# Gate and up in a fixed order by slots, and the second half of each norm placed further behind the first

## The chip, the cores and the metric

One core of a Trainium2 chip runs the whole kernel. The metric is the time of one execution on the device in microseconds (us); the median of several runs counts. Engines are named as the profile names them: PE is TensorE (the matrix multiplier; PEld its weight loads), DVE VectorE, ACT ScalarE, POOL GpSimd, and SP the engine that issues nearly all transfers (SPq is its queue).

## What is computed

One inference step of an encoder layer on 1024 prompt frames and 32 frames of a running stream (1056 columns in all), in fp32, with D_MODEL 1024:

```
x = x + 1/2 * SwiGLU_1(RMSNorm(x))              # FFN1: gate, up, down
h = RMSNorm(x)
q,k,v of 8 stick-breaking heads; q,k,v,r,gate of 4 GLA heads = h @ w_in
o_sb  = rmsnorm(stick_breaking(rmsnorm(q), rmsnorm(k), v))
o_gla = rmsnorm(gated_linear_attention) * silu(r)
x = x + concat(o_sb, o_gla) @ w_out             # the mixer
x = x + 1/2 * SwiGLU_2(RMSNorm(x))              # FFN2
x = RMSNorm(x)

swiglu(h) = (silu(h @ w_gate) * (h @ w_up)) @ w_down        # D_FF = 2816
```

## The kernel before

Each fp32 operand of a large product is split in two: a rounded part "hi" and a remainder "lo" (`split_to`, L94 on ACT makes hi, L98 on DVE makes lo). A product is then three matmuls, hi·hi, hi·lo and lo·hi.

The program runs in stages: FFN1 (an opening in plain products, then gate and up, then down), the mixer, FFN2 in the same form, and the last norm.

**Gate and up.** `gate_up` runs over 20 `Step`s, gate and up of ten row blocks in turn. A Step is a Strassen-Winograd scheme of seven products, taken in `ORDER = (1, 6, 7, 5, 2, 4, 3)`. One product is 24 matmuls of 128x264 (L378) into one of four PSUM accumulators acc_a to acc_d; `after` takes the accumulators out (L391, L394, L397, L416 to L434), and `form`/`keep` (L442, L451) split the hidden rows into forms that are spilled for the down stage. Beside the products of step t the operands of step t+1 are made: `prep` builds the sums S1 to S4 on POOL (L349 to L362) and splits them, `split_w` splits the first weight block ("whl"). Raw weights come by the transfers of L330 and L331.

In FFN1 alone, `Splits` does a chore beside this: 52 half blocks of the mixer's weights (44 of w_in, 8 of w_out) are loaded (L77, 256 KB), split (L94, L98) and stored (L84, 512 KB) for later use. They go through two buffers in turn, S.x[2] and S.x[3]. `keep` uses S.x[0] and S.x[1] in the same manner. The slot of the chore, one product each, is 7·t+n; half block n is loaded at slot 5n//2, split at +3 and stored at +4.

What sets the order of all this is the scheduler of the Tile framework: it takes the instructions that the program emits, estimates when each can start, and writes each engine's queue in its own order. So a chore that stands after a product in the text can lie ahead of or behind it in a queue. On one engine the queue is then executed strictly in order.

**The mixer.** The attention of head pairs p = 0 to 3 is a list of items into which "filler" work is woven, in the order of the list `fill`: for p < 3 the projections of the next pair (`sb_project`: lists pq, pk, pv of three chunks with eight products each), for p = 3 the output groups (`out_group`). A `Norm` has two parts: `stat` squares the rows and sums them on PE into st; then DVE adds epsilon (nv, L756 and L757), POOL takes the power (nr, L759) and copies the result out over 64 rows (L812). `apply` transposes that on PE (tr, L831) and multiplies (L834). `spread_in` puts the three parts of `stat` into a list, and `apply` is put in some places later.

Of the kernel before, what the change touches and what calls it, by code (L numbers as in the profile page):

```python
# [8 lines left out]
F32 = mybir.dt.float32  # L9
F32R = mybir.dt.float32r  # L10
# [44 lines left out]
class Splits:  # L55
# [3 lines left out]
    def __init__(self, S, jobs, bufs):  # L59
        self.S, self.jobs, self.bufs = S, jobs, bufs  # L60
        self.at = {}
        for n in range(2 * len(jobs)):
# [4 lines left out]
    def buf(self, n):  # L67
        return self.bufs[n % 2][:, :1024]

    def halves(self, n):  # L70
        return self.buf(n).rearrange("p (a n) -> p a n", a=2)

    def cols(self, n):
        return slice(n % 2 * 512, n % 2 * 512 + 512)

    def load(self, n):
        self.S.nc.sync.dma_start(self.buf(n)[:, 512:], self.jobs[n // 2][0][:, self.cols(n)])  # L77

    def split(self, n):
        t = self.halves(n).bitcast(F32R)  # L80
        split_to(self.S, t[:, 0], t[:, 1], self.buf(n)[:, 512:])

    def store(self, n):
        self.S.nc.sync.dma_start(self.jobs[n // 2][1][:, :, self.cols(n)], self.halves(n))  # L84

    def some(self, slot):
        for fn, n in sorted(self.at.pop(slot, ()), key=lambda job: job[1]):
            fn(n)

# [227 lines left out]
class Step:  # L317
# [14 lines left out]

    def split_w(self):
        w = self.S.wp.tile([P, 2, 1024], F32R, name="whl", tag="w")
        split_to(self.S, w[:, 0], w[:, 1], self.raw0)
        self.W["A11"], self.W["A12"] = w[:, :, :512], w[:, :, 512:]

    def prep(self, p, eng):

# [105 lines left out]
    def keep(self, name, src):  # L445

        S = self.S
        S.n_kept = getattr(S, "n_kept", 0) + 1
# [17 lines left out]

def gate_up(S, H, op, steps, among, between, tail, xd, chore):


    N = len(steps)  # L470
    done = {}

    def prep(t, p):
        if t >= N:
            return
        steps[t].prep(p, S.nc.gpsimd if t else S.nc.vector)
        done[t] = done.get(t, 0) + 1
        if done[t] == 5 and t + 2 < N:
            steps[t + 2].load()

    for j in range(4):
        for n, i in enumerate((0, 1, 2, 3) if j < 3 else (0, 2, 1, 3)):
            op.product(j, i, among(j, n))
            between(j, n)
            if i == 2:
                op.silu()
            if j == 3 and n == 1:
                steps[0].split_w()
                for p in (6, 7, 5):
                    prep(0, p)  # L490
        op.store(j)
        if j == 1:
            steps[0].load()
            steps[1].load()
    for k in range(4):
        H.part("T3", k, 1)
    for p in (4, 3):
        prep(0, p)
    for t in range(N):
        for p in ORDER:  # L500
            steps[t].product(p)
            steps[t].after(p)
            n = ORDER.index(p)
            for back, name in FORMS[t % 2].get(n, ()):
                if t >= back:
                    steps[t - back].form(name)
            if p > 2:
                prep(t + 1, p)
            if p == 7 and t < N - 1:
                steps[t + 1].split_w()  # L510
            chore(7 * t + n)
            if t == N - 1:
                if p == 1:
                    for d in range(4):
                        S.nc.sync.dma_start(S.x[d], xd[d])
                tail(p)

# [9 lines left out]
class DownStep:  # L527
# [5 lines left out]

    def prep(self, raw):

# [4 lines left out]
        s34 = S.s32.tile([P, 512], F32, name="s34", tag="s2")  # L540
        s1, s2, s3, s4 = s12[:, :w], s12[:, w:], s34[:, :w], s34[:, w:]
        nc.gpsimd.tensor_add(s1, a[3], a[2])
        nc.gpsimd.tensor_sub(s2, s1, a[0])
        nc.gpsimd.tensor_sub(s3, a[0], a[3])
        nc.gpsimd.tensor_sub(s4, a[1], s2)
        tag = ("S1", "A22") if self.odd else ("S2", "S3")
        wa = S.sr.tile([P, 2, 512], F32R, name=tag[0], tag=tag[0])
# [3 lines left out]
        split_to(S, ws[:, 0, :512], ws[:, 1, :512], s12)  # L551
        split_to(S, wb[:, 0, :w], wb[:, 1, :w], a[2])
        split_to(S, ws[:, 0, 512:], ws[:, 1, 512:], s34)
# [42 lines left out]
class Down:  # L596
# [35 lines left out]
    def prep(self, i):  # L632
        if i < len(self.steps):
            self.steps[i].prep(self.raw.pop(i))

    def head(self, p):
# [4 lines left out]
        elif p == 6:  # L641
            for n in range(4):
                self.load_part(0, n)
        elif p == 7:
            self.load_part(0, 4)
            self.load_part(0, 5)
            self.prep(0)
        elif p == 5:
            self.load_part(0, 6)

    def strassen(self, xd):
# [518 lines left out]
def sb_project(S, A, p, norms=()):  # L1170
# [272 lines left out]
def body(tc, A):  # L1443
# [10 lines left out]
    with ExitStack() as top:  # L1454
# [66 lines left out]
        with ExitStack() as es:  # L1521
# [40 lines left out]
            splits = Splits(S, jobs, (S.x[2], S.x[3]))  # L1562
            gate_up(S, H, op, steps, among, between, down.head, A["x"], splits.some)
            nc.vector.tensor_copy(S.identb, consts[:, 0])
# [18 lines left out]
        with ExitStack() as es:  # L1583
# [61 lines left out]
            with ExitStack() as eg:  # L1645
# [16 lines left out]
                for p in range(4):  # L1662
# [3 lines left out]
                    else:  # L1666
# [33 lines left out]
        with ExitStack() as es:  # L1700
# [67 lines left out]

            gate_up(S, H, op, steps, lambda j, n: [], between, down.head, xs, lambda n: None)
            down.strassen(xs)  # L1770
# [111 lines left out]
```

## Time and profile before

| what | value |
|---|---|
| runs | 2164.31, 2160.37, 2160.37 us |
| median | 2160.37 us |
| the profiled execution's own time | 2163.55 us |
| its span, mean granted PE clock | 2161.8 us, 0.987 |
| PE, DVE, ACT, POOL busy | 2067.5, 1454.9, 887.7, 668.8 us |
| gate and up of FFN1, from acc_a's third matmul to the first of down | 84.47 to 524.47 us |
| gate and up of FFN2 | 1497.27 to 1906.82 us |
| attention and output groups of the mixer, roughly | 1000 to 1395 us |

The durations are those of the one profiled execution, whose time is 3.18 us above the median of the runs. A row of a waits view reads "engine tile line <- engine tile line: us in total, times, longest us": the first waits and the second releases it. A row by windows gives a stretch, its length, and for each engine the busy time in it (with the count of instructions), then the granted PE clock (1.00 is full), the share of the DMA engines and GB/s.

### The profile page before, as it was taken

What the parts mean: (1) busy time and instruction counts of PE and PEld (TensorE: products, weight loads), DVE (VectorE), ACT (ScalarE), POOL (GpSimd) and SP (SyncE); (2) the same over time, 40 slices, a digit from 0 to 9 for tenths busy, and PEclk for the clock granted to TensorE, in tenths of its full rate; (3) what the DMA queues carried; (4) which work ended last, traced back from release to release, by engine and by line L of the source; (5) the groups of instructions that cost most, each with busy time, mean ns of one, the idle gap of its engine ahead of it and who ended that gap; (6) DMA issues with size and microseconds to landing.
All of it is one profiled execution on the core that took longest, in us unless ns stands there. A gap on an engine that the chain in (4) does not pass through costs nothing.

```text
span 2161.8 us, 38696 instructions
## 1 busy us (share of the span) xinstructions
PE 2067.5 (96%) x15636; PEld 1997.3 (92%) x15636; DVE 1454.9 (67%) x2205; ACT 887.7 (41%) x1618; POOL 668.8 (31%) x578
## 2 busy tenths in 40 slices
PE   7999988999999999999999998999999999999997
PEld 6898988999999988888889987899999999999997
DVE  6866677664778556376776677687566666457865
ACT  6543444432223333243654555454333433322333
POOL 0133333444775110011112201101343443458720
PEclk9999999999999999999999999999999999999999
DMA  4277777546854121112133243242334334398322
GB/s 173 81 254 259 262 267 269 204 161 249 339 193 125 69 77 59 63 63 85 37 101 98 78 135 106 85 134 80 120 141 156 142 130 160 129 379 299 108 65 81
DMA packets 128339, 325.03 MB, mean 150 GB/s; under 512 B 12096, under 2 KB 32864, under 8 KB 124832
## 3 DMA queue, kind: packets, MB, share of 16 engines
q1 hardware_dynamic: 128160, 322.56, 42.6%
q8 instruction: 123, 2.02, 0.4%
q14 instruction: 56, 0.46, 0.1%
HBM read 201.72 MB, written 114.03 MB: 146 GB/s over the span
## 4 chain that ended last, share of the span: by engine, by line
PE 69%; DVE 11%; DMA 7%; issue 6%; POOL 4%; ACT 3%; SPq 0%; DVEq 0%; ACTq 0%; POOLq 0%
PE acc_a L378 8%; PE acc_d L378 8%; PE acc_c L378 7%; PE acc L286 4%; PE pj L103 4%; PE acc_b L378 4%; PE pj L105 3%; PE pj L104 3%; PE pd_c L574 3%; PE pd_d L574 3%; PE pd_a L574 3%; PE pd L103 2%; PE pd L105 2%; PE pd L104 2%; DMA win_split<-x 2%
## 5 line engine op out<-in xcount | busy, mean ns | idle before, releaser
L378 PE MATMUL acc_a<-h,whl 128*128 128x264 f32 x1920 | 251.4, 287 | 11.5 <-ACT s L391 9.5
L378 PEld LDWEIGHTS acc_a<-h,whl 128*128 128x128 f32 x1920 | 242.3, 191 | 12.9 <-ACT s L391 10.8
L378 PE MATMUL acc_d<-part,S 128*128 128x264 f32 x1920 | 247.3, 284 | 3.7 <-DVE x L418 3.6
L378 PEld LDWEIGHTS acc_d<-part,S 128*128 128x128 f32 x1920 | 238.7, 188 | 4.7 <-DVE x L418 4.3
L94 ACT ACTIVATE x<-x 128x528 fp32r<-128x528 f32 (+1 forms) x164 | 103.4, 638 | 295.8 <-POOL x L428 81.5
L98 DVE TENSOR_TENSOR x<-x 128x528 fp32r<-128x528 f32 (+1 forms) x164 | 132.1, 814 | 132.7 <-ACT x L94 132.0
L103 PE MATMUL pj<-h,whl 128*128 128x352 f32 x576 | 205.3, 356 | 0.0
L105 PE MATMUL pj<-h,whl 128*128 128x352 f32 x576 | 190.9, 331 | 0.0
L104 PE MATMUL pj<-h,whl 128*128 128x352 f32 x576 | 189.3, 329 | 0.0
L94 ACT ACTIVATE S<-s 128x512 fp32r<-128x512 f32 x160 | 98.2, 623 | 114.7 <-PE acc_d L378 43.1
L428 POOL TENSOR_TENSOR x<-tc,x 128x528 f32<-128x528 f32 x60 | 103.3, 1722 | 123.4 <-DVE tc L427 110.7
L362 POOL TENSOR_TENSOR s<-wraw,s 128x512 f32<-128x512 f32 x38 | 49.8, 1312 | 295.2 <-DVE S L98 295.2
L378 PE MATMUL acc_c<-h,A 128*128 128x264 f32 x960 | 126.7, 288 | 10.1 <-DVE u L397 9.8
L378 PEld LDWEIGHTS acc_c<-h,A 128*128 128x128 f32 x960 | 121.8, 190 | 12.3 <-DVE u L397 12.3
L378 PE MATMUL acc_b<-h,S 128*128 128x264 f32 x960 | 124.7, 285 | 1.5 <-ACT h L94 1.1
L98 DVE TENSOR_TENSOR S<-s,S 128x512 fp32r<-128x512 f32 x160 | 120.8, 756 | 6.3 <-ACT S L94 5.6
L378 PE MATMUL acc_c<-part,S 128*128 128x264 f32 x960 | 123.8, 284 | 1.1 <-DVE hid L298 1.1
L378 PEld LDWEIGHTS acc_b<-h,S 128*128 128x128 f32 x960 | 120.5, 188 | 1.9 <-ACT h L94 1.3
L378 PEld LDWEIGHTS acc_c<-part,S 128*128 128x128 f32 x960 | 119.5, 188 | 1.3 <-DVE hid L298 1.3
L592 POOL TENSOR_TENSOR x<-x,u 128x528 f32<-128x528 f32 x64 | 102.9, 1615 | 49.7 <-DVE x L563 49.4
L103 PEld LDWEIGHTS pj<-h,whl 128*128 128x128 f32 x576 | 110.5, 192 | 5.1 <-issue 1.7
L349 POOL TENSOR_TENSOR s<-wraw 128x512 f32<-128x512 f32 x38 | 51.7, 1360 | 201.4 <-DVE S L98 195.2
(343 smaller groups left out, 4952.3 us busy)
## 6 DMA issues: line engine op xcount, KB each, us to landing
part_spill<-x SPq DMA_DIRECT2D x112, 528.0 KB, 2.8
h<-part_spill SPq DMA_DIRECT2D x64, 528.0 KB, 8.9
part<-part_spill SPq DMA_DIRECT2D x48, 528.0 KB, 9.6
win_split<-x SPq DMA_DIRECT2D x44, 512.0 KB, 4.0
whl<-win_split SPq DMA_DIRECT2D x22, 1024.0 KB, 5.0
wraw<-w1g SPq DMA_DIRECT2D x22, 512.0 KB, 4.8
wraw<-w1u SPq DMA_DIRECT2D x22, 512.0 KB, 4.0
x<-win SPq DMA_DIRECT2D x44, 256.0 KB, 3.6
```

Source lines behind the costliest of these rows:

```text
L94: nc.scalar.activation(hi, src, AF.Copy)
L98: nc.vector.tensor_sub(lo, src, hi.bitcast(F32))
L103: nc.tensor.matmul(out, w[:, 0, wsl], a[:, 0, asl], start=first, stop=False)
L104: nc.tensor.matmul(out, w[:, 0, wsl], a[:, 1, asl], start=False, stop=False)
L105: nc.tensor.matmul(out, w[:, 1, wsl], a[:, 0, asl], start=False, stop=last)
L286: nc.tensor.matmul(out, self.w[i](k, a), quarter(S, k, b, j), start=k == 0 and n == 0, stop=k == KT - 1 and n == 2)
L349: eng.tensor_add(self.s1, a21, a22)
L362: eng.tensor_sub(src, a12, self.s2)
L378: nc.tensor.matmul(t[:, s, :SW], w[:, a, ks], m(k, b, s), start=fresh and k == 0 and n == 0, stop=k == 3 and n == 2, skip_group_check=not ...
L428: nc.gpsimd.tensor_mul(two(hid), t, sg)
L574: nc.tensor.matmul(t[:, s, :SW], w[:, u, k * P : k * P + P], b[:, v, ss(s)], start=fresh and k == 0 and i == 0, stop=k == 1 and i == 2, sk ...
L592: nc.gpsimd.tensor_add(x[r][h], x[r][h], u)
```

## The change

1. `Slots` is new. One slot is one product. `Slots.split` puts hi on ACT (L50) into slot k from now, lo on DVE (L51) one slot later, and what follows, a store, one more later. `Slots.run` is called behind each product's `after`.
2. The loop over the Steps now stands in a `manual_schedule` for PE, DVE, ACT, POOL and SP: there each engine's queue is the order of the text, in FFN1 and FFN2.
3. `prep`, `split_w`, `keep` and `Splits` split through the slots: sums one slot later, whl in the same slot, kept parts one slot later with the store at +3; a half block of the chore is loaded at 5n//2, hi at +2, lo at +3, store at +4.
4. The raw weights of step t+2 are loaded at the second product of step t (those of step 2 ahead of the loop), and no longer when five operands of step t are ready.
5. Down's first step makes its sums at product 7 and its halves at product 2 of the last gate/up step, no longer both at 7.
6. In the mixer `apply` of the norm of a head pair goes from pq[1] to pq[2], that of the further norms from pk[2] to pv[0], that of k stays in pv[2] while its `stat` goes from pv[1] to the middle of pv[0]. At p = 3 `apply` (`turned`) goes one place further on (8 for 7), and the nine `ready` splits stand at every second place from 9, no longer at each one from 10.

```diff
+class Slots:
+    def __init__(self, S):
+        self.S, self.now, self.at = S, 0, {}
+    def later(self, k, fn):
+        self.at.setdefault(self.now + k, []).append(fn)
+    def split(self, hi, lo, src, k, then=None):
+        nc = self.S.nc
+        self.later(k, lambda: nc.scalar.activation(hi, src, AF.Copy))
+        self.later(k + 1, lambda: nc.vector.tensor_sub(lo, src, hi.bitcast(F32)))
+        if then is not None:
+            self.later(k + 2, then)
+    def run(self):
+        for fn in self.at.pop(self.now, ()):
+            fn()
...
 class Splits:
-            slot = 5 * n // 2
-            for k, fn in ((0, self.load), (3, self.split), (4, self.store)):
-                self.at.setdefault(slot + k, []).append((fn, n))
...
+            slots.later(k, lambda buf=buf, src=src, cols=cols: dma(buf[:, 512:], src[:, cols]))
+            slots.split(hl[:, 0], hl[:, 1], buf[:, 512:], k + 2, lambda t=t, out=out, cols=cols: dma(out[:, :, cols], t))
...
-        split_to(S, w[:, 0], w[:, 1], src)
+        split(w[:, 0], w[:, 1], src, 1)
...
-        split_to(S, t[:, 0], t[:, 1], src)
-        S.nc.sync.dma_start(S.parts[self.i - 1, PARTS.index(name)], t.bitcast(F32))
+        S.slots.split(t[:, 0], t[:, 1], src, 1, lambda: S.nc.sync.dma_start(out, t.bitcast(F32)))
...
-        if done[t] == 5 and t + 2 < N:
-            steps[t + 2].load()
...
+    steps[2].load()
+    chores(slots)
+    E = mybir.EngineType
+    with S.tc.manual_schedule(engines={E.PE, E.DVE, E.Activation, E.Pool, E.SP}):
+        for t in range(N):
+            for n, p in enumerate(ORDER):
+                steps[t].product(p)
+                steps[t].after(p)
+                slots.run()
+                for back, name in FORMS[t % 2].get(n, ()):
+                    if t >= back:
+                        steps[t - back].form(name)
+                if t < N - 1:
+                    if p > 2:
+                        steps[t + 1].prep(p, S.nc.gpsimd, slots.split)
+                    if p == 7:
+                        steps[t + 1].split_w(slots.split)
+                        slots.run()
+                if n == 1 and t and t + 2 < N:
+                    steps[t + 2].load()
...
+                slots.now += 1
...
     for n in norms[:1]:
-        spread_in(pq[0], 1, 2, n.stat())
-        pq[1][4:4] = [(4, n.apply)]
+        spread_in(pq[0], 0, 3, n.stat())
+        pq[2][4:4] = [(4, n.apply)]
...
     for n in norms[1:]:
         spread_in(pk[1], 0, 3, n.stat())
-        pk[2][4:4] = [(4, n.apply)]
+        pv[0][2:2] = [(4, n.apply)]
...
-    spread_in(pv[1], 0, 3, [(2, start_k), mean_k(1), mean_k(2)])
-    pv[2][2:2] = [(4, lambda: T.nk.apply())]
+    spread_in(pv[0], 4, 3, [(2, start_k), mean_k(1), mean_k(2)])
+    pv[2][0:0] = [(4, lambda: T.nk.apply())]
...
-                        spread_in(fill, 1, 1, prev.stat() + [(4, turned)])
+                        spread_in(fill, 1, 1, prev.stat())
+                        fill.insert(8, (4, turned))
                         for n in range(9):
-                            fill.insert(10 + n, (1, lambda n=n: ready(n // 3, n % 3)))
+                            fill.insert(9 + 2 * n, (1, lambda n=n: ready(n // 3, n % 3)))
```

Three places show what this does to the queues.

The first is ACT in the second Step of FFN1, before. `x_76<-x_76 128x512` is the hi of a chore half block (or, with 128x528, of a kept part), S2, S3, S1 and whl are operands of the next Step, `s1_1125<-acc_a_1100` takes out the Step's first product.

```order
L94 ACTIVATE x_76<-x_76 128x512
L391 ACTIVATE s1_1125<-acc_a_1100 128x528
L94 ACTIVATE S2_1159<-s2_1157 128x512
L94 ACTIVATE x_76<-x_76 128x512
L94 ACTIVATE S3_1193<-s3_1191 128x512
L94 ACTIVATE x_76<-x_76 128x512
L94 ACTIVATE S1_1228<-s1_1155 128x512
L94 ACTIVATE x_76<-x_76 128x528
L94 ACTIVATE whl_1435<-wraw_1095 128x1024
L94 ACTIVATE x_76<-x_76 128x528
L94 ACTIVATE x_76<-x_76 128x512
```

Changed, the same place reads:

```order
L397 ACTIVATE s1_1120<-acc_a_1095 128x528
L50 ACTIVATE x_76<-x_76 128x512
L50 ACTIVATE S4_1094<-s3_1092 128x512
L50 ACTIVATE x_76<-x_76 128x512
L50 ACTIVATE S2_1159<-s2_1157 128x512
L50 ACTIVATE whl_1197<-wraw_872 128x1024
L50 ACTIVATE S3_1196<-s3_1194 128x512
L50 ACTIVATE S1_1232<-s1_1155 128x512
L50 ACTIVATE x_76<-x_76 128x512
L50 ACTIVATE x_76<-x_76 128x528
L50 ACTIVATE A22_1292<-wraw2_873 128x512
L397 ACTIVATE s1_1351<-acc_a_1326 128x528
```

Before, three chores and a kept part stand ahead of, between and behind S2, S3 and S1, the operands of the third Step, and the whl that follows already belongs to the fourth. Now the third Step's whl is made beside S2, and every slot has one operand and one or two splits that end in a store.

The second is PE at the start of FFN1's gate and up, before. acc_a_876 is the first product of the first Step, with the weights whl; acc_b_904 is the second, with S2.

```order
L378 MATMUL acc_a_876<-h0_84,whl_785 128x264 x2
L378 MATMUL acc_b_904<-h0_84,S2_792 128x264 x3
L378 MATMUL acc_b_904<-h1_85,S2_792 128x264 x3
L378 MATMUL acc_b_904<-h2_86,S2_792 128x264 x3
L378 MATMUL acc_b_904<-h3_87,S2_792 128x264 x3
L378 MATMUL acc_b_904<-h0_84,S2_792 128x264 x3
L378 MATMUL acc_b_904<-h1_85,S2_792 128x264 x3
L378 MATMUL acc_b_904<-h2_86,S2_792 128x264 x3
L378 MATMUL acc_b_904<-h3_87,S2_792 128x264 x3
L378 MATMUL acc_c_938<-part0_104,S3_797 128x264
L378 MATMUL acc_a_876<-h0_84,whl_785 128x264
```

Changed:

```order
L384 MATMUL acc_a_878<-h0_84,whl_785 128x264 x3
L384 MATMUL acc_a_878<-h1_85,whl_785 128x264 x3
L384 MATMUL acc_a_878<-h2_86,whl_785 128x264 x3
L384 MATMUL acc_a_878<-h3_87,whl_785 128x264 x3
L384 MATMUL acc_a_878<-h0_84,whl_785 128x264 x3
L384 MATMUL acc_a_878<-h1_85,whl_785 128x264 x3
L384 MATMUL acc_a_878<-h2_86,whl_785 128x264 x3
L384 MATMUL acc_a_878<-h3_87,whl_785 128x264 x3
L384 MATMUL acc_b_906<-h0_84,S2_792 128x264 x3
```

Two of acc_a's 24 matmuls were followed by all 24 of acc_b before acc_a went on; now all of acc_a stand ahead of acc_b.

The third is DVE in the attention of pair 0, in the norm of the next pair's k, before: from the second nv to the first multiplication kf by the transposed result.

```order
L757 TENSOR_SCALAR nv_11076<-st_10975 32x2
L1314 SCALAR_TENSOR_TENSOR f_11088<-f_11088 128x768
L1315 TENSOR_TENSOR w_11089<-w_11089,f_11088 128x768
L98 TENSOR_TENSOR wt_11055<-tr_11108,wt_11055 128x4x128
L834 SCALAR_TENSOR_TENSOR kf_10787<-kf_10787,vec_70,tr_11138 128x512
```

Changed:

```order
L776 TENSOR_SCALAR nv_10988<-st_10953 32x2
L104 TENSOR_TENSOR wt_10997<-tr_10998,wt_10997 128x128
L1305 TENSOR_TENSOR x_76<-avt_11023,av_11006 64x256
L1333 SCALAR_TENSOR_TENSOR f_11026<-f_11026 128x512
L1334 TENSOR_TENSOR w_11027<-w_11027,f_11026 128x512
L104 TENSOR_TENSOR wt_10997<-tr_11040,wt_10997 128x2x128
L1333 SCALAR_TENSOR_TENSOR f_11048<-f_11048 128x640
L104 TENSOR_TENSOR wt_11067<-tr_11068,wt_11067 128x3x128
L1334 TENSOR_TENSOR w_11049<-w_11049,f_11048 128x640
L1305 TENSOR_TENSOR x_76<-avt_11085,av_11080 64x256
L1333 SCALAR_TENSOR_TENSOR f_11091<-f_11091 128x768
L853 SCALAR_TENSOR_TENSOR kf_10790<-kf_10790,vec_70,tr_11118 128x512
```

Three instructions of the attention lay between the two; now there are ten.

More of the change, by code (lines that the diff above doesn't have):

```diff
@@ L60, in __init__, with plan @@
         self.S, self.jobs, self.bufs = S, jobs, bufs
[L61 to L88 removed]
+    def plan(self, slots):
+        for n in range(2 * len(self.jobs)):
+            k = 5 * n // 2
+            buf = self.bufs[n % 2][:, :1024]
+            t = buf.rearrange("p (a n) -> p a n", a=2)
+            hl = t.bitcast(F32R)
+            src, out = self.jobs[n // 2]
+            cols = slice(n % 2 * 512, n % 2 * 512 + 512)
+            dma = self.S.nc.sync.dma_start
+            slots.later(k, lambda buf=buf, src=src, cols=cols: dma(buf[:, 512:], src[:, cols]))
+            slots.split(hl[:, 0], hl[:, 1], buf[:, 512:], k + 2, lambda t=t, out=out, cols=cols: dma(out[:, :, cols], t))
 def split_to(S, hi, lo, src, pool=False):
@@ L464, in gate_up_steps, with gate_up, prep @@
     return steps
-def gate_up(S, H, op, steps, among, between, tail, xd, chore):
+def gate_up(S, H, op, steps, among, between, tail, xd, chores):
     N = len(steps)
[L471 to L477, printed above, removed]
-        if done[t] == 5 and t + 2 < N:
-            steps[t + 2].load()
+    slots = S.slots = Slots(S)
+    now = lambda hi, lo, src, k: split_to(S, hi, lo, src)
+    def prep(p):
+        steps[0].prep(p, S.nc.vector, now)
     for j in range(4):
@@ L497, in gate_up @@
     for p in (4, 3):
[L498 to L516, printed above, removed]
+        prep(p)
+    steps[2].load()
[18 more added lines that the diff above has]
+                    steps[t + 2].load()
+                if t == N - 1:
+                    if p == 1:
+                        for d in range(4):
+                            S.nc.sync.dma_start(S.x[d], xd[d])
+                    tail(p)
+                slots.now += 1
 PAIRS = [(1, 2), (3, 4), (5, 6), (7, 8)]
@@ L532, in __init__, with sums @@
         self.odd = m % 2
-    def prep(self, raw):
+    def sums(self, raw):
         S, nc = self.S, self.S.nc
@@ L1562, in body @@
             splits = Splits(S, jobs, (S.x[2], S.x[3]))
-            gate_up(S, H, op, steps, among, between, down.head, A["x"], splits.some)
+            gate_up(S, H, op, steps, among, between, down.head, A["x"], splits.plan)
             nc.vector.tensor_copy(S.identb, consts[:, 0])
@@ L1767, in between @@
                     emit(parts(H))
-            gate_up(S, H, op, steps, lambda j, n: [], between, down.head, xs, lambda n: None)
+            gate_up(S, H, op, steps, lambda j, n: [], between, down.head, xs, lambda slots: None)
             down.strassen(xs)
```

25 lines of the change are left out of this document (17 added, 8 removed).

## The prediction

> **What bounds the kernel now.** I read the page first, then the time by windows, then who waits for whom in the windows that fall short. TensorE carries the kernel:
>
> ```profile
> span 2161.8 us, 38696 instructions
> PE 2067.5 (96%) x15636; PEld 1997.3 (92%) x15636; DVE 1454.9 (67%) x2205; ACT 887.7 (41%) x1618; POOL 668.8 (31%) x578
> ```
>
> The change reorders and removes no matmul, so it can win at most what PE idles or runs at a reduced granted clock. Where that lies, the windows tell: gate and up of FFN1 while the chores run, the rest of it, the same work in FFN2, and short stretches around stalls.
>
> ```profile
> core 0: us, PE busy (x) PEld busy (x) DVE busy (x) ACT busy (x) POOL busy (x), PEclk, DMA share, GB/s
> 100.00:377.00 277.00, 254.62 (x2021) 250.22 (x2019) 192.85 (x250) 115.03 (x195) 103.30 (x66) 0.99 0.74 262
> 377.00:495.00 118.00, 117.07 (x959) 117.03 (x960) 73.57 (x95) 43.11 (x70) 49.93 (x33) 1.00 0.48 173
> 1497.27:1906.82 409.55, 409.55 (x3361) 409.55 (x3360) 251.21 (x325) 149.77 (x240) 164.35 (x115) 1.00 0.41 149
> 140.00:145.00 5.00, 3.04 (x17) 3.04 (x18) 4.00 (x7) 3.24 (x7) 1.49 (x2) 0.80 0.68 249
> 230.00:235.00 5.00, 4.32 (x23) 4.33 (x24) 4.95 (x9) 3.36 (x7) 0.00 (x0) 0.68 0.57 219
> 85.00:90.00 5.00, 5.00 (x31) 5.00 (x30) 5.00 (x9) 0.61 (x1) 1.28 (x1) 0.66 0.18 62
> ```
>
> FFN2 is the measure: 3360 matmuls in 409.55 us with no PE idle, 0.1219 us each and 2.925 us for a product of 24 (a slot). At that pace the 2021 matmuls from 100 to 377 take 246.3 us; they took 277.0. Of the 30.7 us lost, 22.4 are idle (277 − 254.6) and 8.3 are matmuls at a reduced clock, as the rows at 140 and 230 show (0.80, 0.68). After the chores the loss is 118 − 959 × 0.1219 = 1.1 us. So the chores cost it. Who waits between 110 and 377:
>
> ```profile
> DVE x L98 <- ACT x L94: 73.9, 33, 4.4
> ACT x L94 <- DMA x<-win: 54.0, 22, 5.9
> ACT x L94 <- POOL x L428: 29.6, 9, 3.7
> PE acc_c L378 <- DVE u L397: 9.8, 8, 2.3
> PE acc_a L378 <- ACT s L391: 9.5, 6, 2.0
> PE acc_d L378 <- DVE x L418: 2.5, 2, 1.3
> ```
>
> PE waits 21.8 us for accumulators to be taken out; ACT and DVE are late with that because a chore stands ahead of it in their queues: ACT stands 54.0 us at a hi whose load has not landed, DVE 73.9 us at the lo behind it. The chain of waits from 150 to 240 shows one link after another of this:
>
> ```profile
> 154.58 4.20 DMA x<-win
> 158.88 0.64 ACT x L94
> 159.55 0.70 DVE x L98
> 160.26 3.02 DMA win_split<-x
> 163.35 4.52 DMA x<-win
> ```
>
> **Part 1, chores by slots (FFN1).** How tight is the new timetable? The rows of the chores, with the median times to landing from the page:
>
> ```profile
> L98 DVE TENSOR_TENSOR x<-x x96: 675/697/1840, 98.8 to 399.8; 128x512 fp32r<-128x512 f32 x52, 128x528 fp32r<-128x528 f32 x44
> L77 SPq DMA_DIRECT2D x<-win x44: 327/333/846, 88.9 to 340.9; - x44
> L77 SPq DMA_DIRECT2D x<-wo x8: 327/330/847, 344.4 to 385.1; - x8
> win_split<-x SPq DMA_DIRECT2D x44, 512.0 KB, 4.0
> x<-win SPq DMA_DIRECT2D x44, 256.0 KB, 3.6
> ```
>
> One turn of a buffer is load 3.6, hi 0.64, lo 0.70, store 4.0: 8.9 us. Before, 52 loads in two buffers were issued from 88.9 to 385.1, 51 steps of 5.81 us, 11.6 us for a turn. The new timetable gives 5 slots, 14.6 us, so it has 3.0 us to spare against the old turn and 5.7 against the sum. From a load's slot to its hi are two slots, 5.85 us for 3.6 (longest single wait 5.9). The chores then last until slot 131 (5 × 51 // 2 + 4), 383 us instead of some 300.
>
> The other queues: SP keeps its order of text; a chore's load waits for the store one slot ahead (4.0 us, of which one slot is past), and the kept parts' stores behind it are delayed by 1 us, with two slots before their buffer is used again. The weights of step t+2 go out at the second product of step t, when the last reader of their buffers (the sums and lo's of step t) is a slot old. POOL takes the sums in order, at 164 of 410 us busy in FFN2. DVE gets 52 × 0.70 = 36 us on top of FFN2's 251.2: 70% of 409.6. An accumulator is used again two products later, so an evacuation may be one slot late before PE notices. I find no queue that the order overfills.
>
> Price: if FFN1 ran as FFN2, 30.7 + 1.1 = 31.8 us would go. Restart and entry come off:
>
> ```profile
> 75.88 1.26 PE L378 MATMUL acc_b<-h,S 128*128 128x264 f32 x9
> 84.47 1.92 PE L378 MATMUL acc_a<-h,whl 128*128 128x264 f32 x9 [1.99 <-DVE whl L98]
> 524.47 1.62 PE L574 MATMUL pd_a<-h,S 128*128 128x264 f32 x12
> 506.01 6.30 SPq L620 DMA_DIRECT2D h<-part_spill  x8
> ```
>
> Entry: whl is done at 84.47 in both (DVE's order up to there is the same), but the 24 matmuls of acc_b, which before ran while PE waited for it, now stand behind acc_a: 24 × 0.1219 = +2.9 us (bounds 0, if whl came as much sooner, and 3.2). The clock after that wait was 0.66 anyway (85 to 90). So at best 31.8 − 2.9 = 28.9 us go. The same by the whole stage: 524.47 − 84.47 = 440.0 against 409.55 leaves 30.4, less 1.7 for the restart at 0.66 (5 us × 0.34): 28.7.
>
> The tail: eight loads of spilled parts went out at 506.01 and PE entered down at 524.47 without a wait. The four loads of x now come right ahead of them, as the chores end later: 0 to 4 us, taken as 1. For DVE or ACT being late here and there I keep 2.7: two stalls like those at 140 and 230, where idle and clock together cost 1 to 2 us each. FFN1: −25, between −28.7 and half of the loss, −15.
>
> **Part 2, gate and up of FFN2.** No chores, no idle PE, and matmuls in the same order: 0. What can be lost is bounded by one stall per pair of Steps, 10 × 0.8 us: +8. It cannot gain.
>
> **Part 3, the norms in the mixer.** The waits from 1000 to 1395, the first and the second stall from the waits of their own windows, the rows of the norm's chain, and by windows what follows the first and second stall, a stretch without any, and the last stall with what follows it:
>
> ```profile
> PE tr L831 <- POOL x L812: 12.7, 5, 5.8
> PE tr L831 <- POOL x L812: 2.6, 1, 2.6
> PE tr L831 <- POOL x L812: 1.1, 1, 1.1
> L759 POOL TENSOR_TENSOR nr<-nv,mhalf x11: 1797/3218/5297, 1010.0 to 1320.2; 128x18 f32<-128x18 f32 x9, 128x9 f32<-128x9 f32 x2
> L812 POOL COPY x<-nr x6: 1036/1036/1714, 1070.3 to 1325.5; 128x1024 f32<-128x1024 f32 x6
> 1071.30:1076.00 4.70, 4.65 (x21) 4.21 (x22) 3.54 (x4) 0.00 (x0) 0.30 (x3) 0.64 0.00 0
> 1167.20:1172.20 5.00, 4.59 (x31) 4.08 (x32) 5.00 (x6) 0.36 (x2) 0.99 (x3) 1.00 0.00 0
> 1210.00:1250.00 40.00, 39.56 (x278) 37.77 (x278) 23.79 (x42) 21.12 (x47) 7.26 (x11) 1.00 0.15 54
> 1321.00:1326.60 5.60, 0.00 (x0) 0.00 (x0) 3.24 (x4) 0.00 (x0) 5.54 (x3) 0.77 0.00 0
> 1326.60:1332.00 5.40, 5.37 (x21) 4.27 (x21) 2.85 (x6) 2.05 (x4) 0.24 (x2) 0.60 0.17 45
> ```
>
> Behind the last sum the chain is power 3.2 and copy 1.0, with DVE's nv ahead of it; five transposes came before it was done. The matmuls between a norm's last sum and its first transpose go, in the queue, from 27 to 68 (pair 0, k), 37 to 84 (pair 1), 27 to 51 (pair 1, k), 31 to 70 (pair 2) and 20 to 41 (pair 2, k); with 39.56 / 278 = 0.142 us each the extra 21 to 47 give 3.0 to 6.7 us, more than the stalls there (12.7 − 5.8 = 6.9 us for the four, the longest 2.6). They go, and with the longest the low clock behind it (0.64 over 4.7 us: 1.7). At p = 3 the power took 5.3 us and PE stood 5.8; there the matmuls go from 50 to 62, 12 × 0.142 = 1.7 us of it, and the clock stays low. Sum −10.3. Against it: the transposes move to where DVE is behind with the attention's own, so I take −9. Bounds: 0, if the wait only changes its name, and −16.6, if all 12.7 and the low clock behind both long stalls (1.7 and 5.4 × 0.40 = 2.2) go.
>
> **Sum** against the profiled execution's 2163.55: −25 + 0 − 9 = 2129.5. The median of the runs lies 3.2 below that execution, so 2126.
>
> **A rule on the clock.** The rows show a reduced clock after short stalls: 0.68 and 0.80 in windows whose single idle stretches were at most 2.3 us, 0.64 after one of 2.6, but 1.00 after one of 1.1. The Trainium skill ("TensorE: Matmul & The Clock Gate", Part 1: The HAM clock gate) says that the clock falls to half only after an idle window of about 3.4 us that runs freely. By that rule stalls this short would cost nothing but themselves. The rows here disagree with it in part. What the rule would make of the time is rival C.
>
> **Rivals.**
> A. The slots take away half of the stalls: an evacuation still stands behind a hi in some slots, as loads land late (5.9 us was the longest wait of ACT, just the two slots given). FFN1 −13, mixer −9: 2138. The DMA share falls with the chores spread (0.74 at 262 GB/s now), which speaks against it.
> B. The mixer gives nothing: the transposes then stand before DVE, and a wait for DVE takes the place of that for POOL. FFN1 −25 alone: 2135.
> C. The reduced clock of FFN1 has another cause than the stalls and stays: of the 30.7 us the 8.3 remain, and in the mixer 1.7: 2136. The clock of 1.00 in FFN2, with no stall, speaks against it.
> D. Slower. In a fixed order one late link, load to hi to lo to store to load, stops ACT and with it every evacuation, in each slot. It paces PE when a turn of a buffer exceeds 5 slots, 14.6 us; to lose more than 4.3 in all, FFN1 must lose 9 + 4.3 and take 453 us, so the slots with chores must grow from 2.925 to (453 − 9 × 2.925) / 131 = 3.26 and the turn to 16.3 us, against 11.6 measured. At 17 us the 131 slots take 3.4 us each: 445 + 26 = 472 instead of 440, with the entry's 3 and the mixer's −9 +26: 2186.
> E. The change doesn't do what it says in FFN1, since the stalls come from late data and not from the order; FFN1 0, FFN2 0 to +8, mixer −9: 2151 to 2159. That ACT and PE lose nothing in FFN2, where no load is split, would fit this too.
>
> **How the numbers follow.** Chances: forecast 0.65, A 0.08, B 0.10, C 0.05, D 0.06, E 0.06. A difference of 0.2%, 4.3 us, is about what a measurement of this kernel can tell from none. D is slower; E is split, 0.02 faster and 0.04 the same; the others are faster: 0.90, 0.04, 0.06. The forecast's own range: best −28.7 and −16.6 give 2115, worst −15 and −2 give 2143. With A, B and C inside, and D and E left out (0.12), the range is 2116 to 2146.
>
> **What would show it.** Right: 140 products of FFN1 in 410 to 416 us at a clock near 1.00, waits of PE for L397 and L403 under 4 us there, and loads of chores every 7.3 us up to about slot 127; acc_b's first matmul some 3 us behind acc_a's; four of the five waits of tr gone and the last near 4 us; FFN2 at 409 to 411 us. Wrong: PE waits in FFN1 that recur every slot (D), waits of tr for DVE in place of POOL (B), windows without idle at a clock of 0.9 (C), or a stretch of idle at 500 to 530 us before down.

## The result, and the profile after

The changed kernel takes 2135.5 us (median of four runs, 2132.5 to 2136.3) against 2162.3 for the kernel before beside it: a ratio of 0.9872, 95% interval 0.9855 to 0.9890. It is 27 us faster. The forecast was 34 us (2126 us, range 2116 to 2146). Its profiled execution takes 2135.43 us, 28.1 less than that of before.

The page and the windows of the changed kernel, the counterparts of those shown before (gate and up of FFN1 now run from 85.22 to 496.90, those of FFN2 from 1467.80):

```profile
span 2133.5 us, 38802 instructions
PE 2058.4 (96%) x15636; PEld 1991.8 (93%) x15636; DVE 1438.7 (67%) x2205; ACT 886.8 (42%) x1618; POOL 655.3 (31%) x578
...
100.00:377.00 277.00, 277.00 (x2274) 277.00 (x2273) 202.60 (x262) 122.38 (x203) 110.76 (x74) 1.00 0.68 241
377.00:495.00 118.00, 118.00 (x970) 118.00 (x969) 77.53 (x104) 47.95 (x80) 46.28 (x34) 1.00 0.76 272
495.00:530.00 35.00, 34.98 (x287) 34.76 (x286) 21.57 (x28) 8.34 (x16) 20.86 (x20) 1.00 1.00 379
85.22:496.90 411.68, 411.68 (x3359) 411.68 (x3360) 290.62 (x379) 174.80 (x291) 162.80 (x113) 0.99 0.69 247
```

In 277 us PE does 2274 matmuls instead of 2021, without a gap and at full clock. The whole stage takes 411.7 us, where the same products in FFN2 take 410. PE waits just once in it, at the entry:

```profile
PE acc_a L384 <- DVE whl L104: 8.4, 1, 8.4
```

The chores now go out up to 465.7 instead of 385.1, and ACT waits less for their loads: 22.7 us in 13 waits for win and wo, where from 110 to 377 alone the loads of win cost it 54.0 us before. The rows of line 93 with the first and last start of a load, and ACT's waits for loads from 100 to 485:

```profile
L93 SPq DMA_DIRECT2D x<-win x44: 327/334/1452, 89.6 to 401.7; - x44
L93 SPq DMA_DIRECT2D x<-wo x8: 328/330/337, 410.7 to 465.7; - x8
ACT x L50 <- DMA x<-win: 12.9, 10, 5.8
ACT x L50 <- DMA x<-wo: 9.8, 3, 7.1
```

Of the five waits of the norm's transposes for POOL one is left, the last; waits for DVE of 1 to 2 us have come in with the new places. PE's waits from 1000 to 1346:

```profile
PE tr L1345 <- DVE wt L104: 3.4, 5, 1.5
PE tr L850 <- POOL x L831: 3.2, 1, 3.2
PE tr L850 <- DVE wt L104: 2.7, 3, 2.1
PE tr L850 <- DVE kf L853: 1.8, 2, 1.0
```

Stage by stage, each from the start of its first matmul to that of the next stage (or of its own last), in us, for three kernels and a second execution of the changed one:

| stage | before | changed | again | mixer alone changed |
|---|---|---|---|---|
| FFN1 gate and up, first acc_a to first pd_a | 448.9 | 420.5 | 420.9 | 448.4 |
| FFN1 down, to the first pd | 171.1 | 174.6 | 174.5 | 171.0 |
| rest of down, GLA, to the first z | 318.1 | 318.6 | 317.6 | 320.7 |
| attention, to the last av | 363.5 | 355.3 | 354.9 | 353.0 |
| last output groups, to the last po | 72.5 | 75.0 | 72.0 | 71.8 |
| FFN2 opening, gate and up, to the last acc_d | 457.0 | 457.4 | 457.0 | 457.0 |
| FFN2 down, to the last pd of h and part | 240.6 | 241.2 | 241.6 | 239.7 |

FFN1's gate and up gives 28 us and the attention 8; down of FFN1 takes 3.5 back, and in this execution the last output groups take 2.5.

### The profile page after: what moved, and what is told of

Same layout as the page of the kernel before. It is cut to its first block, busy times and chain, and to the rows that moved or that the text cites. A ratio compares the mean times of both kernels' runs of the same rounds, so it can differ in the third digit from the quotient of the medians.

```text
span 2133.5 us, 38802 instructions
## 1 busy us (share of the span) xinstructions
PE 2058.4 (96%) x15636; PEld 1991.8 (93%) x15636; DVE 1438.7 (67%) x2205; ACT 886.8 (42%) x1618; POOL 655.3 (31%) x578
## 4 chain that ended last, share of the span: by engine, by line
PE 80%; DVE 9%; issue 3%; DMA 3%; ACT 3%; POOL 2%; DVEq 0%; SPq 0%; ACTq 0%; POOLq 0%
PE acc_a L384 11%; PE acc_c L384 11%; PE acc_d L384 11%; PE acc_b L384 6%; PE acc L292 4%; PE pj L109 4%; PE pj L111 3%; PE pj L110 3%; PE pd_a L590 2%; PE pd_d L590 2%; PE pd_c L590 2%; PE pd L109 2%; PE pd L111 2%; PE pd L110 2%; DMA wraw<-hid_spill 2%
## 5 line engine op out<-in xcount | busy, mean ns | idle before, releaser
L50 ACT ACTIVATE x<-x 128x528 fp32r<-128x528 f32 (+1 forms) x164 | 102.5, 635 | 113.8 <-issue 30.2
L51 DVE TENSOR_TENSOR x<-x 128x528 fp32r<-128x528 f32 (+1 forms) x164 | 129.9, 805 | 17.4 <-ACT x L50 17.4
L355 POOL TENSOR_TENSOR s<-wraw 128x512 f32<-128x512 f32 x38 | 58.1, 1529 | 225.9 <-DVE S L104 186.4
L109 PEld LDWEIGHTS pj<-h,whl 128*128 128x128 f32 x576 | 109.8, 191 | 4.8 <-issue 1.5
L50 ACT ACTIVATE S<-s 128x512 fp32r<-128x512 f32 x152 | 93.4, 623 | 46.9 <-PE acc_b L384 18.4
L51 DVE TENSOR_TENSOR S<-s,S 128x512 fp32r<-128x512 f32 x152 | 112.1, 738 | 0.0
L111 PEld LDWEIGHTS pj<-h,whl 128*128 128x128 f32 x576 | 109.2, 190 | 1.9 <-issue 1.0
```

The costliest lines, as they stand in the source:

```text
L50: self.later(k, lambda: nc.scalar.activation(hi, src, AF.Copy))
L51: self.later(k + 1, lambda: nc.vector.tensor_sub(lo, src, hi.bitcast(F32)))
L109: nc.tensor.matmul(out, w[:, 0, wsl], a[:, 0, asl], start=first, stop=False)
L111: nc.tensor.matmul(out, w[:, 1, wsl], a[:, 0, asl], start=False, stop=last)
L355: eng.tensor_add(self.s1, a21, a22)
```

## The experiments

Kernels that were measured together share their chip and the runs of the kernel before; those runs lie between 2156 and 2166 us, so a difference of 2 to 3 us between single medians says little, and what decides below is mostly the stage in the profile.

**Gate and up alone** (the four edits in the mixer undone):

```diff
-        spread_in(pq[0], 0, 3, n.stat())
-        pq[2][4:4] = [(4, n.apply)]
+        spread_in(pq[0], 1, 2, n.stat())
+        pq[1][4:4] = [(4, n.apply)]
```

> The change's gate and up (slots, fixed order, down's first step), with the mixer as before. Theory: the whole of FFN1's gain and the loss of down's start stand here: from the first acc_a to the first pd 27 to 28 us less, down 3 to 4 us more, the mixer as before, in all -24 us against before. Rival (the 3.5 us in down and the 2 to 3 us in the last output groups are chance of one execution): -27 to -28.

Measured: 2137.8 against 2161.6 us, −23.9, ratio 0.9891 (0.9876 to 0.9906). FFN1's gate and up 420.4 us, its down 175.3 (171.1 before), the attention 363.1 as before. The loss in down belongs to the change of gate and up, though no line of down's steps after the first differs.

**The mixer alone** (the reverse: those edits put into the kernel before).

> The change's mixer alone, gate and up as before. Theory: attention gives 8 us, the last output groups give 2 to 3 back: -5 us. Rival by the prediction's sum: -9. Rival by the median of the whole change (what is left beside FFN1's 27.6 is nothing): 0 to -1.

Measured: 2153.3 us, −8.3, ratio 0.9962 (0.9947 to 0.9976); the attention 353.0, the output groups 71.8 and down 171.0 us. The prediction's −9 stands. The output groups lose nothing here, and the second execution of the changed kernel has 72.0 there: the 75.0 of the first was that one execution, in which PE waited 4.4 instead of 1.2 to 1.5 us for whl.

**The fixed order without the new spacing** (hi and lo of a split in one slot, as in the text of before; the earlier loads of the raw weights and the new places of down's first step stay):

```diff
-            slots.split(hl[:, 0], hl[:, 1], buf[:, 512:], k + 2, lambda t=t, out=out, cols=cols: dma(out[:, :, cols], t))
+            slots.later(k + 3, lambda hl=hl, buf=buf: split_to(slots.S, hl[:, 0], hl[:, 1], buf[:, 512:]))
+            slots.later(k + 4, lambda t=t, out=out, cols=cols: dma(out[:, :, cols], t))
...
-        S.slots.split(t[:, 0], t[:, 1], src, 1, lambda: S.nc.sync.dma_start(out, t.bitcast(F32)))
+        split_to(S, t[:, 0], t[:, 1], src)
+        S.nc.sync.dma_start(out, t.bitcast(F32))
...
-                        steps[t + 1].prep(p, S.nc.gpsimd, slots.split)
+                        steps[t + 1].prep(p, S.nc.gpsimd, now)
```

> The changed kernel with the text order of before: gate and up in the fixed order, but hi and lo of a split in one slot, operands and kept parts split at once, chores loaded at 5n//2, split at +3, stored at +4. Theory (it is the fixed order with the chores at 5n//2 that takes the stalls away): PE idle under 2 us between the second Step and the first pd, time within 3 us of the changed kernel. Rival (the slot between hi and lo does it): half of FFN1's stalls come back, +10 to +15 us against the changed kernel.

Measured: 2129.3 us (2126.9 to 2137.5). The stage by windows:

```profile
84.60:496.00 411.40, 411.30 (x3358) 411.30 (x3359) 300.16 (x380) 173.65 (x290) 167.88 (x113) 1.00 0.70 244
```

Behind the entry PE waits for nothing in it. At the lo's of chores and kept parts DVE now waits 52.8 us in 59 waits for ACT's hi (7.4 in 8 in the changed kernel), and that costs PE nothing. So the slot between hi and lo is worth nothing here; the fixed order, which lets no chore run ahead of its place, is enough to take the stalls away. The loads of the raw weights, which also moved, were not tried alone; in the kernel before no engine waits for one between 110 and 377.

**The entry** (the first Step's lo of whl on POOL, which idles there):

```diff
-                steps[0].split_w(now)
+                steps[0].split_w(lambda hi, lo, src, k: split_to(S, hi, lo, src, True))
```

> The changed kernel with the lo of the first Step's whl (in FFN1 and FFN2) made on POOL instead of DVE. Theory (at the start of gate and up PE idles 8.4 us for that one lo, which stands far back in DVE's queue, and pays a clock of one half for 10 us with it): acc_a goes on at once at 76.4, acc_b and acc_c then wait 3 to 4 us for DVE, in all -6 us against the changed kernel (-4.5 to -7.5). Rival (DVE's whole backlog is what counts, the wait moves to acc_b and acc_c): 0 to -2.

Measured: 2130.7 us, 1.8 under the second median of the changed kernel, on another chip; the first pd_a comes at 494.3 instead of 496.9. PE at the start:

```profile
76.19 3.09 PE L384 MATMUL acc_a<-h,whl 128*128 128x264 f32 x24
79.12 1.52 PE L384 MATMUL acc_b<-h,S 128*128 128x264 f32 x10
81.25 1.97 PE L384 MATMUL acc_b<-h,S 128*128 128x264 f32 x14 [0.61 <-DVE h L104]
84.34 0.39 PE L384 MATMUL acc_c<-part,S 128*128 128x264 f32 x1 [1.11 <-DVE hid L304]
88.74 1.47 PE L384 MATMUL acc_c<-part,S 128*128 128x264 f32 x5 [4.02 <-DVE part L104]
```

acc_a runs at once and acc_b nearly so, and acc_c waits for DVE instead, up to 88.7: 5.7 us of waits in place of 8.4. The stall was for the most part not one lo but DVE's backlog, as the rival had it; the expected −6 became −2.6.

**The changed kernel again.**

> The changed kernel unaltered, beside the others on one chip. Theory: its parts add up, -23.9 (gate and up alone) and -8.3 (mixer alone) give -32, the -26.8 of its first four runs was low by chance: -29 to -32 us. Rival (the two parts disturb each other, -26.8 is the true value): -25 to -28.

Measured: 2132.5 against 2160.4 us, −27.9, ratio 0.9873 (0.9853 to 0.9892). The two parts alone give 0.9891 and 0.9962, together 0.985; its interval overlaps that of the whole. Whether some 4 us get lost between them stays open; 2 of them would be in the attention (353.0 us alone, 354.9 here).

**Without the loads of x** (the last Step's four loads left out, so down adds to stale rows).

> The changed kernel with the four loads of x in the last gate/up Step of both FFNs left out (so down adds to stale rows). In the queues the down stage of FFN1 then has PE's order of the kernel before, and DVE's but for 12 rows. Theory (the 3.5 us that down loses come from the order in which the scheduler lays down, which hangs on its estimate of when x is there): first pd_a to first pd 171 to 172.5 us instead of 174.6. Rival (the loads of x and the chores before them delay the loads of the parts, and the order is the same in effect): the loads issued earlier, but pd_c and pd_d wait as before: 174 to 175.

Measured: 2128.9 us; down of FFN1 174.1 us, no better. With no load of x ahead of the parts, and PE's order that of the kernel before, PE waits 6.6 us for pd_c in six places instead of the 4.4 in three of that kernel. Neither the loads nor PE's order make the loss. Of the queues of PE and DVE, what differs still from before are 12 places in DVE's, which led to the experiment on down.

**Chores closer together**: three slots for a turn of a buffer, and four, instead of five.

```diff
-            k = 5 * n // 2
+            k = 3 * n // 2
...
-            slots.split(hl[:, 0], hl[:, 1], buf[:, 512:], k + 2, lambda t=t, out=out, cols=cols: dma(out[:, :, cols], t))
+            slots.split(hl[:, 0], hl[:, 1], buf[:, 512:], k + 1, lambda t=t, out=out, cols=cols: dma(out[:, :, cols], t))
```
```diff
-            k = 5 * n // 2
+            k = 2 * n
```

> The changed kernel with the chores at three slots for a turn of a buffer instead of five (load at 3n//2, hi one slot later, lo and store at +2 and +3), in FFN1's first 80 slots: 8.8 us for a turn whose parts sum to 8.9. Theory (in a fixed order the turn paces PE as soon as it exceeds its slots, and with nothing queued ahead it takes some 9.5 us): those slots take 3.2 instead of 2.925 us, +15 to +25 us against the changed kernel, with PE waiting for ACT and DVE in nearly every slot. Rival 1 (the turn takes the 11.6 us of before): +70. Rival 2 (the evacuations have slack enough, PE never waits): 0.

> The changed kernel with the chores at four slots for a turn (load at 2n), done by slot 106; a load then waits for a store issued in its own slot, 4.0 + 3.6 us for two slots of 5.85. PE's order in the down stage of FFN1 is that of the kernel before. Theory: PE idle between the second Step and the first pd under 3 us, since an accumulator may be taken out a slot late, and down 171 to 172.5 us instead of 174.6: -2 to -4 us against the changed kernel. Rival (a late hi delays evacuations at once): PE waits 10 us or more for L397 and L403, +8 to +15.

Measured: 2216.3 us with three slots, 2191.1 with four: 84 and 59 us slower than the changed kernel, and slower than the kernel before (ratios 1.025 and 1.0133, intervals 1.0233 to 1.0267 and 1.0116 to 1.0151). The first expectation was far too low (its rival of 70 us, with the old turn of 11.6, came nearest), and the second had the wrong sign. With four slots, the stage from 100 to 458, and who waits (SP from 100, ACT and DVE from 90, to 450; PE from 100 to 458):

```profile
100.00:458.00 358.00, 320.58 (x2487) 315.58 (x2486) 203.47 (x287) 135.25 (x225) 108.98 (x78) 0.96 0.64 218
SPq L93 <- DMA win_split<-x: 219.0, 44, 9.1
ACT x L50 <- DMA x<-win: 142.0, 40, 8.3
DVE x L51 <- ACT x L50: 131.9, 73, 7.9
PE acc_c L384 <- DVE u L403: 19.2, 6, 3.6
```

It is the chain of rival D: SP stands at a load until the store of the same buffer has landed (5 us on average, up to 9.1), all later stores and loads stand behind it, ACT stands at the hi, and the evacuations stand behind that. PE is idle for 37.4 of these 358 us, 19.2 of them for acc_c and the rest for acc_a and acc_d, and the clock falls to 0.96. In gate and up the 106 slots with chores take (558.7 − 496.9) / 106 = 0.58 us more each, 3.51 us, so a turn takes 14.0 us for the 11.7 it was given; with three slots it takes 12.0 for 8.8, worked out in the same way over 80 slots (down begins at 582.5). The changed kernel gives it 14.6. Why the turn is shorter with three slots than with four stays open. With four, down takes 175.3 us and not the 171 to 172.5 expected, though PE's order there is that of the kernel before.

**Down in the fixed order** (twelve of its sixteen steps, one pair of halves behind each of four products):

```diff
+        manual = S.tc.manual_schedule(engines={E.PE, E.DVE, E.Activation, E.Pool, E.SP})
+        manual.__enter__()
...
+                if st.g < last:
+                    nx = self.steps[i + 1]
+                    if n == 1:
+                        nx.sums(self.raw.pop(i + 1))
+                        nx.halves(True)
+                    if 2 <= n < 6:
+                        nx.one()
```

DVE's queue in the third step of down, in the changed kernel, where the scheduler sets the order:

```
L579 SCALAR_TENSOR_TENSOR x_76<-pd_a_5880,x_76 128x528
L104 TENSOR_TENSOR S1_5920<-wraw2_5771,S1_5920 128x512
L104 TENSOR_TENSOR whl_5922<-s12_5914,whl_5922 128x512
L104 TENSOR_TENSOR A22_5921<-wraw2_5771,A22_5921 128x256
L104 TENSOR_TENSOR whl_5922<-s34_5915,whl_5922 128x512
L579 SCALAR_TENSOR_TENSOR x_76<-pd_c_5931,x_76 128x528
```

Four lo's stand ahead of pd_c's evacuation. Before, in the same step, two stood singly and two together; in this experiment all four stand singly between evacuations. PE's waits in down, in the kernel before and in the changed one:

```profile
PE pd_c L574 <- DVE tc L563: 4.4, 3, 1.9
PE pd_c L590 <- DVE tc L579: 3.6, 2, 1.9
PE pd_d L590 <- DVE x L579: 2.3, 2, 2.1
PE pd L109 <- DVE x L579: 1.1, 1, 1.1
```

With 0.3 for pd_d before and 0.2 for another wait of the changed kernel they are 4.7 and 7.2 us. The other 1.0 of the 3.5 is busy time of PE (167.4 instead of 166.4 us); from 524 to 545 the clock is 0.92 in the changed kernel.

> The changed kernel with the first twelve of the sixteen steps of down in the fixed order too, each of the four pairs of halves of the next step behind another product. Theory (down loses its 3.5 us because the scheduler puts up to four lo's in a row ahead of one evacuation on DVE): first pd_a to first pd 167 to 169 us instead of 174.6, and 4 to 6 us less in FFN2's down: -9 to -12 us against the changed kernel. Rival (DVE and POOL hold each other up in down, whatever the order): 173 to 175 us, 0 to -2.

Measured: 2126.3 us, ratio 0.9843 (0.9828 to 0.9859). Down of FFN1 takes 171.3 us, as in the kernel before, with this left of its waits:

```profile
PE pd_c L598 <- DVE tc L587: 4.1, 2, 2.5
497.80:669.10 171.30, 166.06 (x1346) 165.42 (x1344) 119.62 (x173) 53.16 (x93) 113.50 (x107) 0.99 0.65 237
```

FFN2's down takes 239.6 instead of 241.6. Setting the order ends the loss. The experiment fixes all queues at once, so that DVE's is the one is argued and not shown by itself: it rests on the waits (PE waits in down for DVE alone) and on the experiments without the loads of x and with four slots, where PE's order in down was that of before, DVE's was not in 12 places, and the loss stayed. That it would go on to 167 to 169 was too much: two waits stay.

**The last norm's apply further on** (10 for 8). It then comes behind the first output group that adds to x[4], which is loaded again only behind it, so part of that sum is lost.

```diff
-                        fill.insert(8, (4, turned))
+                        fill.insert(10, (4, turned))
...
-                            fill.insert(9 + 2 * n, (1, lambda n=n: ready(n // 3, n % 3)))
+                            fill.insert(11 + 2 * n, (1, lambda n=n: ready(n // 3, n % 3)))
```

> The changed kernel with the apply of the last pair's norm two places further on (10 instead of 8) and the ready splits with it. Theory (at p = 3 the transposes still come 3.2 us before POOL's copy, and the clock is at one half for 6.8 us behind that): wait gone, -3 to -6 us against the changed kernel. Rival (the wait goes to DVE or to the out groups, which then follow late): 0 to -1.

Measured: 2131.3 us, 1.3 under the second median of the changed kernel. The wait for POOL is gone and the attention takes 350.6 us instead of 354.9, with a new wait of 1.9 us for DVE; the stages ahead of it happened to be longer in this execution (495.5 us from the first pd_a to the first z, 492.1 in the second execution of the changed kernel). By the stage the theory holds; by the time it can't be told from nothing.

**All three together** (with that same loss in x[4]), and the same with the apply at 9, where nothing is lost.

> The changed kernel with the first Step's lo on POOL, down in the fixed order and the last norm's apply two places further on. If the parts add up: -4.8 -10 -4, about -19 us against the changed kernel, 2113 to 2118 us.

> As the combination of all three, but the last norm's apply one place further on (9 instead of 8) with the ready splits from 10 on: the last place at which the reloading of x still stands ahead of the output groups that add to it. Theory: POOL's copy is then waited for by 3.2 less one output group (12 matmuls of 0.14), about 1.5 us, with a low clock behind it: 2120 to 2123 us, 10 to 12 less than the changed kernel. Rival (the last norm's wait falls on no path that counts): the same as the combination, 2121.

Measured: 2120.9 us, ratio 0.9814 (0.9800 to 0.9827), and 2123.5 us, ratio 0.9832 (0.9815 to 0.9850). The latter beats both kernels: 9 us under the second median of the changed one, 36.7 under the one before. The three parts did not add up to 19: against that second median they give 11.6, as the entry gave 2.6 and not 4.8, down 6.3 and not 10, and the norm 1.3 and not 4. With the apply at 9 the wait of 1.5 us for POOL that was expected to stay is gone too; the time lies just above the 2120 to 2123 expected.

## Why the prediction was right, and where its sum was off

Against the profiled execution it said −34 and got −28.1. Its mechanism was right in both parts. That the time came as near as it did is partly luck: gate and up of FFN1 gave 3.4 us more than forecast, and that hid the 3.5 us that down lost, for which the sum had no term. By its own steps:

**Chores by slots.** −25 was forecast, with entry and tail in it. It is −28.4 from the first acc_a to the first pd_a, close to the best case. The 3.7 kept for the tail and single stalls were not needed: PE enters down at 496.9 without a wait though the DMA engines are full (share 1.00 at 379 GB/s from 495 to 530). Entry: acc_b did move behind acc_a (90.1 against 75.9), as forecast, but it comes 4.9 us after acc_a goes on at 85.2 and not 3, as PE runs at about half clock there (0.52 from 85 to 90).

**The cause.** The window and the chain named it, and the fixed order removed it without the new spacing. With that rivals A and E, half of the stalls or all of them left, are out; so is C, as the clock is 1.00 from 100 to 377. The part of the argument that sized the slack was wrong, though it did no harm: "11.6 us for a turn", "3.0 us to spare against the old turn and 5.7 against the sum". A turn is not the sum of its landings. SP's queue, in order, waits for each store, and with four slots the 12 stores that overlap a transfer of raw weights take 7.9 us to land on average, the other 32 take 4.7. Given 11.7 us the turn takes 14.0. In the changed kernel too SP stands at such loads, 111.9 us in 43 waits for stores of win in gate and up; there it keeps PE waiting for nothing. Rival D, held to decide at 16.3 us a turn and given 6 in 100, was the right mechanism and lay one slot away.

**Gate and up of FFN2.** 0 forecast, +0.4 measured.

**Norms.** −9 forecast, −8.2 in the attention here and −8.3 for the mixer alone: four waits gone (6.9 us), the last one 2.6 us shorter (3.2, where the sum had left 4.1 of it), and the low clock behind it kept. PE's idle time in the attention falls by 7.6 us, from 23.9 to 16.3, so about 2 us of other waits, for DVE in the main, came in for the 1.3 that the sum took off; and PE's busy time falls by 0.6 instead of the 1.7 that it took for the clock. Rival B (nothing gained) is out.

**What failed** is the step that isn't there: the sum had no term for down. It priced down at its entry, and took the rest as untouched, because the diff leaves the order there to the scheduler. But behind the fixed part the scheduler laid DVE's queue otherwise (how it comes to do so was not followed): +3.5 us in FFN1's down. The queues show it beforehand, when they are compared there as well. The other 2.5 us, in the last output groups, were chance of one execution; a single profiled execution carries some 3 us of it.

**The clock.** The prediction wrote that the rows disagree in part with the Trainium skill's rule ("TensorE: Matmul & The Clock Gate", Part 1: The HAM clock gate). In the main they don't; its 5 us windows blurred them. Cut at 3.41 us in the kernel before, ahead of and behind two stalls in gate and up, and behind the first in the mixer:

```profile
139.59:143.00 3.41, 1.15 (x9) 1.04 (x9) 3.32 (x6) 1.33 (x3) 0.41 (x1) 1.00 0.86 342
143.00:146.40 3.40, 3.40 (x18) 3.40 (x17) 1.83 (x4) 2.97 (x5) 2.47 (x2) 0.50 0.59 180
228.30:231.70 3.40, 1.46 (x12) 1.25 (x11) 3.31 (x5) 2.22 (x5) 0.53 (x1) 1.00 0.09 33
231.70:235.10 3.40, 3.40 (x18) 3.40 (x17) 3.40 (x6) 1.66 (x3) 0.00 (x0) 0.51 0.86 333
1071.42:1074.83 3.41, 3.41 (x14) 3.04 (x14) 2.38 (x2) 0.00 (x0) 0.18 (x3) 0.51 0.00 0
```

The clock is 0.50 or 0.51 for one stretch of 3.41 us, and full (0.99 to 1.00) in those ahead of it and behind it. The stretches lie on one grid: the second of those at half clock begins 26 stretches after the first, the third 272. The window of 3413 ns, free-running, and the two states of which the Trainium skill speaks there agree with that. What it calls an idle window was here one in which PE was still busy for 1.15 or 1.46 of 3.41 us. Where a wait lies on the grid then decides what it costs. Five waits between 100 and 377 are about 2 us long. The first two (in brackets in these rows, which give start and length of the matmuls behind a wait) each fall into one stretch, and their 24 matmuls take 4.7 us. The other three, with one of 1.99 us at 369.64, lie across the edge of two stretches, and their 24 matmuls take 3.2:

```profile
141.96 4.72 PE L378 MATMUL acc_c<-h,A 128*128 128x264 f32 x24 [2.26 <-DVE u L397]
230.68 4.71 PE L378 MATMUL acc_a<-h,whl 128*128 128x264 f32 x24 [1.94 <-ACT s L391]
276.96 3.20 PE L378 MATMUL acc_a<-h,whl 128*128 128x264 f32 x24 [2.00 <-ACT s L391]
327.74 3.21 PE L378 MATMUL acc_c<-h,A 128*128 128x264 f32 x24 [2.08 <-DVE u L397]
```

A stretch at half clock costs 1.7 us, and these two are the only ones from 100 to 377, so they explain 3.4 of the 8.3 us that the prediction put down to the clock there. The other 4.9 come with the stops as well: PE stops 19 times in that time, and each stop leaves about 0.26 us more that counts as busy. The first matmul behind it takes 0.39 us instead of 0.28 and the next starts 0.23 us after it instead of 0.12, and of the last one ahead of it 0.16 us are not overlapped by another; 19 times 0.26 is 4.9.

## What to carry to other kernels

Where chores share queues with the work that bounds the kernel, a fixed place for each can be worth more than space between the steps of one (here 28 us against nothing); but in a fixed order the whole chain, waits of the issuing queue for its own stores included, must fit its slots, and the margin is found by giving it one slot less, not by adding up landing times: one slot less cost 59 us here. When part of a program is taken out of a scheduler's hands, compare the queues of what comes behind as well: it may be laid out anew. And before a wait is costed as one late instruction, look whether the engine behind it is simply full: then the wait moves and does not go.

## What the runs showed of the hardware that was not expected

A load issued by SP behind a store of the same buffer holds up all that SP issues next: with four slots SP stood 219 of the 350 us from 100 to 450 there.

In gate and up one stretch of 3.41 us in which PE is about 60% idle (1.15 to 1.46 us busy) is followed by exactly one at half clock, 1.7 us lost; with 1.76 us busy, from 323.91 to 327.32, none followed. The wait of 1.1 us at 1166 left the clock at 1.00 and cost 1.1, while 2.3 us of idle in one stretch cost 4. The busy time of the profile alone does not tell it, though. In the mixer of the kernel before PE was busy for 3.08 us of a stretch and the next ran at half clock; 2.1 us of that were 18 matmuls of a single column each. What is counted there no run here shows:

```profile
1006.57:1009.98 3.41, 3.08 (x25) 2.76 (x24) 2.93 (x8) 2.28 (x4) 0.00 (x0) 1.00 1.03 300
1009.98:1013.39 3.41, 3.41 (x14) 3.27 (x13) 0.77 (x2) 0.27 (x1) 1.91 (x2) 0.51 0.78 152
```
